# Hybrid decoder trunk on one core: the low part of one weight split per gate/up pair by an adding DMA

## The chip, the cores and the metric

The kernel runs on 1 core of one Trainium2 chip. The metric is device time of one execution in microseconds (us); the median of several runs is given. Engines are named as in the profile: PE (matmul) with PEld (its weight loads), DVE (vector), ACT (scalar), POOL (GpSimd), SP (which issues the DMAs of the kernel before).

## The reference

A two-layer decoder trunk in float32, run for a prompt of 512 tokens and for 8 samples of 8 tokens that share all weights, 576 token columns in all. Layer 0 mixes by causal pooling, layer 1 by a gated DeltaNet; each mixer is followed by a SwiGLU block:

```python
def swiglu(h, w_in, w_out):
    gu = h @ w_in
    return (jax.nn.silu(gu[..., :D_FF]) * gu[..., D_FF:]) @ w_out

for i in range(DEPTH):                      # DEPTH = 2, D_MODEL = 1024, D_FF = 2816
    h = rms_norm(x, norm_mix_pre[i])
    m = pool_mixer(...) if i % 2 == 0 else gdn_mixer(...)
    x = x + rms_norm(m, norm_mix_post[i])
    h = rms_norm(x, norm_ffn_pre[i])
    x = x + rms_norm(swiglu(h, ffn_w_in[i], ffn_w_out[i]), norm_ffn_post[i])
```

The outputs are the trunk's result for prompt and samples and the new states of both mixers.

## The kernel before

**Splits.** Every large matmul is done three times in a rounded 32-bit type (fp32r): a value x is held as a high part (x rounded to fp32r) and a low part (x less the high part), and the products high·high, high·low and low·high are summed. So each weight block is loaded (SP), copied to its high part (ACT) and subtracted to its low part (DVE or POOL, whichever the planner picks: `EITHER`). `split2` does it for two given tiles, `Weights.split` for tiles that it allocates.

**The gate/up pairs.** In each SwiGLU block, f runs over 22 blocks of 128 hidden columns. The first few (6 in layer 0, 5 in layer 1) are computed directly by `gate_up`; the other 33 (16 and 17) by the class `Strassen`, which takes the gate block and the up block of one f together, in seven products of half size. `Strassen.load` loads both 128x1024 weight blocks into tiles g (`graw`, two buffers) and u (`wraw`, three), forms sums of their halves, and splits three blocks of 128x1024 and one of 128x512: g itself to a (`wh`, `wl`), the half sum `s1raw` to s, then g after it was overwritten with two sums to b (tiles `dh` and `dl`, two buffers each), and u with its sum to c. `gated` runs the seven products in the order g1, g2, s2, s1, s3, s4, u2; s2 and s4 read b. Each product is 12 matmuls of 288 columns. In the profile the low part of b is the group `dl<-graw,dh`, the high part `dh<-graw`, and PE's use of them `ps_A<-ta,dl`, `ps_B<-hH,dh` and the like. Runs of pairs alternate with output projections: blocks of 6, 5, 4, 7 in layer 0 and 5, 5, 5, 7 in layer 1, where the first block is the direct one.

**The order of the work.** The program first records every operation in `Plan`. `Plan.cost` gives a planning price for each: how long it holds its engine, and when its result is there. `Plan.forward` then places the operations in time, engine by engine, by rank; where PE would be idle for long it inserts filling matmuls (`ps_w`). `Plan.refined` walks through the plan in windows of 60000 planned ns, in steps of 30000, and shifts ranks at random by the seeds that the constant `CHOSEN` lists for the window (`moved`); a string of `CHOSEN` is one such walk. The instructions are then emitted in the planned order. On the chip each engine runs its own instructions in that order and waits on semaphores, so the seeds fix the order on every engine, SP's DMA issues too. In the profile nearly all instructions have the one line that emits them; they are told apart by their tiles.

**Stretches** of the profiled execution, by the tiles in work: to about 100 us the pooling mixer, then layer 0's SwiGLU block with its pairs from 140 to 405, the DeltaNet layer from 440 to 1045, then the projection of its output and layer 1's direct blocks, its pairs from 1185 to 1455, and the end.

Of the kernel before, what the change touches and what calls it, by code (L numbers as in the profile page):

```python
# [20 lines left out]
P = 128  # L21
# [38 lines left out]
class Plan:  # L60
# [683 lines left out]
def hybrid_kernel(  # L744
# [147 lines left out]
    class Weights:  # L892
# [4 lines left out]
        def load(self, src, row, col, nk, n=P, eng=EITHER):  # L897
            raw = self.p.tile([P, 8, P], F32, name="wraw", tag="wraw", bufs=self.raw)[:, :nk, :n]
            SP.dma_start(raw, src[row:row + nk * P, col:col + n].rearrange("(k p) m -> p k m", p=P))
            return self.split(raw, eng)  # L900
# [1270 lines left out]
```

## Time and profile before

| what | value |
|---|---|
| median of 3 runs | 1513.48 us (1512.61 to 1514.94) |
| profiled execution, first to last instruction | 1513.1 us |
| granted clock of PE, mean | 0.997 |
| DMA share of the 16 engines, queue of SP | 45.1% |
| DMA packets of queue POOL | none |

The profiled execution's span lies 0.4 us below the median of the runs and inside their range. In the rows below, "busy" is the time in which an engine ran instructions (waiting and DMA issuing are not counted). A row of a group reads: line, engine, operation, tile written <- tiles read, shapes, count | busy us, mean ns of one | idle time of the engine just before, and what ended it. A row of the timeline reads: start us, us, engine, operation, tiles, and in brackets the idle time before it. Matmuls overlap, so a matmul's own duration is longer than the distance from one to the next.

### The profile page before, as it was taken

The numbers are of one execution on the slowest core, as the hardware profiler recorded it, in microseconds if no ns is written. First come the engines' busy times: TensorE is split into PE (matmuls) and PEld (weight loads), VectorE is DVE, ScalarE is ACT, GpSimd is POOL, SyncE is SP. The second block draws the span as 40 slices with busy tenths as digits, with TensorE's granted clock in tenths as the row PEclk, the third lists the DMA queues.
The fourth block names the chain that finished last, engine by engine and source line by source line (L and its number), as shares of the span: only waits on it lengthen the run. The fifth ranks groups of instructions, "written<-read, shape, count | busy, mean of one in ns | idle before, by whom it ended". The sixth has DMA issues, their size and how long they took to land.

```text
span 1513.1 us, 30285 instructions
## 1 busy us (share of the span) xinstructions
PE 1492.6 (99%) x11786; PEld 1446.6 (96%) x11786; DVE 1134.2 (75%) x2289; ACT 853.6 (56%) x1841; POOL 106.8 (7%) x240
## 2 busy tenths in 40 slices
PE   8999999999999999999999999999999999999998
PEld 7999999999999899899899899999999999999997
DVE  7993566668789697897899789557896485767856
ACT  7753443435555875774694784645565453533555
POOL 4100000000011010110121030000110000000000
PEclk9999999999999999999999999999999999999999
DMA  7564333233466443334443544657865332233264
GB/s 198 171 173 114 87 91 95 75 98 111 124 180 186 108 116 112 105 101 132 127 116 101 152 113 123 212 149 212 249 187 168 112 97 86 81 93 114 69 166 136
DMA packets 344934, 198.12 MB, mean 131 GB/s; under 512 B 13515, under 2 KB 337708, under 8 KB 344783
## 3 DMA queue, kind: packets, MB, share of 16 engines
q1 hardware_dynamic: 344791, 196.18, 45.1%
q8 instruction: 93, 1.52, 0.4%
q14 instruction: 50, 0.41, 0.1%
HBM read 165.86 MB, written 30.52 MB: 130 GB/s over the span
## 4 chain that ended last, share of the span: by engine, by line
PE 86%; DVE 6%; ACT 3%; DMA 3%; issue 1%; POOL 0%; SPq 0%; DVEq 0%; ACTq 0%; POOLq 0%
PE ps_A L462 27%; PE ps_B L462 26%; PE ps_m L462 19%; PE ps_s L462 5%; PE ps_k L462 5%; PE ps_x L462 2%; PE ps_e L462 1%; DVE wl L462 1%; DMA xt<-in_x_prompt_dram 1%; PE ps_n L462 1%; DVE y L462 1%; ACT wh L462 1%; DVE nacc L462 1%; PE ps_g L462 0%; ACT QD L462 0%
## 5 line engine op out<-in xcount | busy, mean ns | idle before, releaser
L462 DVE TENSOR_TENSOR wl<-wraw,wh 128x1024 fp32r<-128x1024 f32 (+4 forms) x238 | 266.2, 1123 | 76.4 <-ACT wh L462 47.3
L462 ACT ACTIVATE wh<-wraw 128x1024 fp32r<-128x1024 f32 (+4 forms) x239 | 232.4, 977 | 155.0 <-PE ps_B L462 65.3
L462 PE MATMUL ps_m<-hH,wh 128*128 128x320 f32 (+1 forms) x832 | 252.0, 315 | 0.7 <-ACT zz L462 0.4
L462 PE MATMUL ps_m<-hH,wl 128*128 128x320 f32 (+1 forms) x832 | 247.2, 309 | 0.0
L462 PE MATMUL ps_m<-hL,wh 128*128 128x320 f32 (+1 forms) x832 | 245.8, 306 | 0.1
L462 PEld LDWEIGHTS ps_m<-hH,wh 128*128 128x128 f32 x832 | 154.7, 189 | 4.1 <-ACT u L462 0.9
L462 PEld LDWEIGHTS ps_m<-hL,wh 128*128 128x128 f32 x832 | 155.3, 189 | 2.4 <-issue 0.8
L462 PEld LDWEIGHTS ps_m<-hH,wl 128*128 128x128 f32 x832 | 154.5, 189 | 2.7 <-issue 1.1
L462 PE MATMUL ps_B<-hL,wh 128*128 128x288 f32 (+2 forms) x444 | 129.1, 306 | 0.0
L462 PE MATMUL ps_B<-hH,wl 128*128 128x288 f32 (+2 forms) x444 | 128.4, 306 | 0.2
L462 PE MATMUL ps_B<-hH,wh 128*128 128x288 f32 (+2 forms) x444 | 128.4, 305 | 0.0
L462 PE MATMUL ps_A<-hH,wl 128*128 128x288 f32 (+2 forms) x432 | 117.9, 289 | 0.2
L462 PE MATMUL ps_A<-hH,wh 128*128 128x288 f32 (+2 forms) x432 | 117.4, 288 | 0.3 <-ACT nsq L462 0.3
L462 PE MATMUL ps_A<-hL,wh 128*128 128x288 f32 (+2 forms) x432 | 117.1, 288 | 0.0
L462 PE MATMUL ps_A<-aH,wl 128*128 128x288 f32 (+2 forms) x408 | 114.5, 297 | 0.0
L462 PE MATMUL ps_A<-aH,wh 128*128 128x288 f32 (+2 forms) x408 | 114.2, 298 | 0.0
L462 PE MATMUL ps_A<-aL,wh 128*128 128x288 f32 (+2 forms) x408 | 113.7, 296 | 0.0
L462 PE MATMUL ps_B<-aH,wl 128*128 128x288 f32 x296 | 83.3, 297 | 0.0
L462 PE MATMUL ps_B<-aH,wh 128*128 128x288 f32 x296 | 82.7, 295 | 0.3 <-ACT nsq L462 0.3
L462 PEld LDWEIGHTS ps_B<-hH,wl 128*128 128x128 f32 x444 | 81.8, 188 | 0.8 <-DVE wl L462 0.7
L462 PE MATMUL ps_B<-aL,wh 128*128 128x288 f32 x296 | 82.6, 294 | 0.0
L462 PEld LDWEIGHTS ps_B<-hL,wh 128*128 128x128 f32 x444 | 81.9, 188 | 0.1
(457 smaller groups left out, 3966.1 us busy)
## 6 DMA issues: line engine op xcount, KB each, us to landing
wraw<-in_ffn_w_in_dram SPq DMA_DIRECT2D x77, 512.0 KB
wraw<-in_gdn_w_in_dram SPq DMA_DIRECT2D x56, 512.0 KB
graw<-in_ffn_w_in_dram SPq DMA_DIRECT2D x33, 512.0 KB
wraw<-in_ffn_w_out_dram SPq DMA_DIRECT2D x32, 448.0 KB
wraw<-in_gdn_w_out_dram SPq DMA_DIRECT2D x24, 512.0 KB
wraw<-in_ffn_w_out_dram SPq DMA_DIRECT2D x32, 320.0 KB
St<-in_state_gdn_rec_dram SPq DMA_DIRECT2D x32, 256.0 KB
out_dram<-St SPq DMA_DIRECT2D x32, 256.0 KB
```

What stands on the lines that cost most here:

```text
L462: calls[e](*a, **k)
```

## The change

`split3` is new: ACT writes the negated high part (a copy with scale -1, rounded to fp32r) into the low tile, then the high part into the high tile, and POOL issues a DMA that reads the source and adds it onto the low tile. The subtraction on DVE is gone. `Strassen.load` uses `split3` in place of `split2` for b, the block in `dh` and `dl`. `Weights.load` and `Weights.split` take a new argument `adds` that nothing sets. `Plan.cost` gets a price for a DMA issued by POOL. `CHOSEN` is replaced: 6 strings with 4926 seeds in place of 4 strings with 2045.

```diff
     CHOSEN = (
-        "0: 30370 22361 86136 57126 4872 4820 4237 36728 5998 9791 48895 50747 41137; 1: 45223 42774 67949 96695 "
...
     )
...
         if method == "dma_start":
             m = n * list(out.ap)[0][1]
             flat = len(list(out.ap)) == 2
+            if eng == "POOL":
+                return 1000.0, 2500.0 + m * 4 / 240.0
...
-        def load(self, src, row, col, nk, n=P, eng=EITHER):
+        def load(self, src, row, col, nk, n=P, eng=EITHER, adds=False):
             raw = self.p.tile([P, 8, P], F32, name="wraw", tag="wraw", bufs=self.raw)[:, :nk, :n]
             SP.dma_start(raw, src[row:row + nk * P, col:col + n].rearrange("(k p) m -> p k m", p=P))
-            return self.split(raw, eng)
-
-        def split(self, raw, eng=EITHER):
+            return self.split(raw, eng, adds)
+
+        def split(self, raw, eng=EITHER, adds=False):
...
-            ACT.activation(h, raw, AF.Copy)
-            eng.tensor_tensor(l, raw, h.bitcast(F32), op=sub)
+            if adds:
+                split3(raw, h, l)
+            else:
+                ACT.activation(h, raw, AF.Copy)
+                eng.tensor_tensor(l, raw, h.bitcast(F32), op=sub)
             return h, l
...
+    def split3(src, hi, lo):
+
+        ACT.activation(lo, src, AF.Copy, scale=-1.0)
+        ACT.activation(hi, src, AF.Copy)
+        POOL.dma_start(lo, src, accum_op=add)
...
             b = tuple(ap_.tile([P, 8, P], F32R, name="d" + x, tag="d" + x, bufs=2) for x in "hl")
-            split2(g, *b)
+            split3(g, *b)
             c = w.split(u)
```

425 rows, old and new, of the table CHOSEN are left out of this document.

## The prediction

> **What bounds the kernel now.** I read the page's busy shares first, then busy time by stretch, then the chain, then single pairs of blocks in the timeline.
>
> ```profile
> span 1513.1 us, 30285 instructions
> PE 1492.6 (99%) x11786; PEld 1446.6 (96%) x11786; DVE 1134.2 (75%) x2289; ACT 853.6 (56%) x1841; POOL 106.8 (7%) x240
> ```
>
> TensorE is the bound; VectorE, which the change relieves, stands at 75%. Shares of a whole span hide stages, so here are stretches (window, its length, busy us and instructions of PE, PEld, DVE, ACT, POOL, granted clock, DMA share, GB/s):
>
> ```profile
> 0.00:100.00 100.00, 94.00 (x717) 89.45 (x718) 87.15 (x213) 71.69 (x158) 27.30 (x82) 1.00 0.67 185
> 140.00:405.00 265.00, 265.00 (x1997) 264.59 (x1996) 176.79 (x272) 116.28 (x179) 0.00 (x0) 1.00 0.31 90
> 440.00:1045.00 605.00, 598.11 (x5085) 560.71 (x5084) 492.97 (x1195) 400.38 (x1082) 64.67 (x142) 1.00 0.47 135
> 1045.00:1185.00 140.00, 139.79 (x1053) 138.48 (x1053) 106.45 (x195) 78.64 (x134) 11.47 (x12) 1.00 0.66 198
> 1185.00:1455.00 270.00, 270.00 (x2037) 269.75 (x2036) 187.14 (x289) 120.86 (x184) 0.00 (x0) 1.00 0.32 93
> 1455.00:1513.10 58.10, 50.73 (x380) 48.85 (x378) 34.47 (x58) 30.14 (x55) 0.00 (x0) 0.95 0.56 158
> ```
>
> The 33 gate/up pairs that the change touches lie in 140 to 405 and 1185 to 1455. PE is busy there for 265.00 of 265 and 270.00 of 270 us, 132.7 ns per matmul (265/1997); DVE is busy 67% and 69%, ACT 44% and 45%, POOL not at all. Where DVE is relieved, PE doesn't wait for it. PE's idle time is elsewhere: 6.0 us at the start, 6.9 us in the DeltaNet stretch (605 - 598.11), 7.4 us at the end, where the last transposes, norms and stores follow one another.
>
> ```profile
> 9.70 15.43 DMA xt<-in_x_prompt_dram
> 444.71 6.26 DMA wraw<-in_gdn_w_in_dram
> 1148.16 5.67 DMA wraw<-in_ffn_w_in_dram
> ...
> L458 PE MATMUL ps_w<-ones 128*128 128x128 f32 x86 | 13.9, 307 | 1.3 <-POOL ones L237 1.3
> ```
>
> The first three are pieces of the chain (start, us): a wait for the input at the start, and two waits for one 512 KB weight block. The last is a filling matmul, 86 of them, 13.9 us: PE time that is a wait too.
>
> **The change, part by part.** (Against 1513.1 us of span; the three runs have a median of 1513.48, so 0.4 us are added to the span.)
>
> ```profile
> L462 DVE TENSOR_TENSOR dl<-graw,dh 128x1024 fp32r<-128x1024 f32 x33 | 40.3, 1221 | 10.7 <-ACT dh L462 10.6
> L462 ACT ACTIVATE dh<-graw 128x1024 fp32r<-128x1024 f32 x33 | 34.8, 1054 | 31.1 <-DVE graw L462 29.1 <-PE ps_A L462 2.0
> q1 hardware_dynamic: 344791, 196.18, 45.1%
> ```
>
> 1. Removed: 33 subtractions of 1.221 us, 40.3 us of DVE. Worth 0: PE stands over them, idle 0.00 us in both stretches.
> 2. Added on ACT: 33 negated copies, the same copy as dh with a scale, so 33 x 1.054 = 34.8 us, 16 of them in the first stretch and 17 in the second: ACT rises from 116.3 to 133.2 of 265 and from 120.9 to 138.8 of 270. Cost 0, covered by ACT's idle half. They stand ahead of dh on ACT's queue, so dh is 1.05 us later, and the copies that free PSUM may queue behind them.
> 3. Added on POOL and the DMA engines: 33 adds of 512 KB. The DMA engines spent 45.1% of 1513.1 = 682 us on 196.18 MB, 3.48 us per MB, thus 1.8 us for 0.524 MB, 3.6 if the old value is read as well; 16 x 3.6 = 58 us lift the share in the first stretch from 0.31 to 0.53. PE loses 0.21 of 140 us where the share is 0.66, so this bandwidth costs 0.
> 4. How long one add takes isn't in the trace: no DMA is issued by POOL. From below it is bounded by what it replaces, 1.2 us. From above by the longest landing, 6.26 us, plus POOL's slowest small instruction beside a busy DVE:
>
> ```profile
> L462 POOL TENSOR_TENSOR sqs<-qks x10: 395/650/2034, 603.5 to 874.3; 128x128 f32<-128x128 f32 x10
> L462 POOL MEMSET Rs<- x4: 952/952/956, 589.5 to 950.4; 128x1024 f32 x4
> ```
>
> that is 6.26 + 2.03 = 8.3 us. I take 4.7 us, which is also the planner's price in the diff (2500 + 524288/240 ns): it lies above the bare 1.8 to 3.6 us and below the 5.67 us of a load in a stretch with twice the DMA traffic.
> With it dl comes 1.05 + 4.7 - 1.22 = 4.5 us later than now (1.0 at the low end, 8.1 at the high end). What waits for it:
>
> ```profile
> 282.40 1.22 DVE L462 TENSOR_TENSOR dl<-graw,dh 128x1024 fp32r<-128x1024 f32 x1
> 284.26 0.19 PEld L462 LDWEIGHTS ps_B<-ta,dl 128*128 128x128 f32 x1
> ...
> 361.42 1.06 ACT L462 ACTIVATE dh<-graw 128x1024 fp32r<-128x1024 f32 x1 [3.17 <-DVE graw L462]
> 362.63 1.22 DVE L462 TENSOR_TENSOR dl<-graw,dh 128x1024 fp32r<-128x1024 f32 x1
> 363.88 0.37 SPq L462 DMA_DIRECT2D graw<-in_ffn_w_in_dram  x1
> 363.91 0.19 PEld L462 LDWEIGHTS ps_A<-ta,dl 128*128 128x128 f32 x1
> 375.73 1.06 ACT L462 ACTIVATE wh<-graw 128x1024 fp32r<-128x1024 f32 x1 [0.26 <-PE ps_A L462]
> ...
> 1415.85 1.23 DVE L462 TENSOR_TENSOR dl<-graw,dh 128x1024 fp32r<-128x1024 f32 x1 [0.19 <-ACT dh L462]
> 1425.60 0.19 PEld L462 LDWEIGHTS ps_A<-hH,dl 128*128 128x128 f32 x1
> ```
>
> Three pairs: dl is done 0.64, 0.06 and 8.5 us before PE's first load of it. The order is just in time, so a late dl shows at once unless the new order starts it earlier. Room for that is there: d has two buffers, and between the last product that reads one pair's d (s4) and the first that reads the same buffer again (s2, two pairs on) stand ten products of 12 matmuls (u2, the seven of the pair between, g1, g2), 10 x 12 x 0.1327 = 15.9 us; copy, copy and add take 1.05 + 1.05 + 4.7 = 6.8. At 8.3 us it is 10.4, still inside. Cost 0 if the order uses it.
> 5. SP's queue: the next load into graw is issued when dl has read it (363.85, issue at 363.88); that release goes from DVE to the add's landing. The block loaded there is first read at 375.73, 11.9 us after the issue, and a landing takes up to 6.3 us, so 5.6 us are to spare against 4.5. Behind the waiting issue stand SP's other loads:
>
> ```profile
> SPq L462 <- DVE dl L462: 113.8, 18, 13.8
> ```
>
> SP waits for dl 18 times already, up to 13.8 us, with PE full. Cost 0, but this is the second thinnest cover. On POOL nothing queues behind the adds: it has no instruction in either stretch.
> 6. New seeds: the whole order is drawn again, everywhere. They can't win in the pair stretches. What an order can win is waits: 6.0 + 6.9 us idle and 13.9 us of filling, 26.8, less the 15.4 us of the input's wait: 11.4 us. They can lose as much as a bad order leaves, which the trace doesn't show. There are 4926 seeds for 2045, so I take a gain of a third, 3.8 us, between nothing and 11.4.
>
> Sum: 0 + 0 + 0 + 0 + 0 - 3.8: span 1509.3, time about 1509.5.
>
> **The rivals.**
> B: the adds are hidden and the order is worth nothing on the chip. For it: PE at 99%. Against: 11.4 us of waits are left. 1513.
> C: the adds land later than the order allows for, and PE stalls in the pair stretches. For it: two of the three leads above are under 0.7 us; the sqs row shows POOL work stretched five times (395 to 2034 ns). Against: the memset on POOL, which reads nothing, is even (952 to 956 ns). Six runs of pairs (blocks of 5, 4, 7 and 5, 5, 7) follow one another with projections between; once PE is late in a run, the rest of that run is no longer late. Between an overshoot of 0 and 8.3 - 4.7 = 3.6 us I take 1.8, less a lead of 0.4: 6 x 1.4 = 8 us, so 1513.5 + 8 = 1521 without a gain elsewhere, 1518 with it; I say 1519. It decides once the add overshoots by more than 3.8/6 + 0.4 = 1.0 us, at 5.7 us.
> The Trainium skill (SBUF — State Buffer, "SBUF: two separate sides") says that VectorE in a two-port mode locks GpSimd out of writing descriptors, with a DMA stretched from about 620 to 3100 ns; by that each add would be some 2.5 us late (an estimate from that page) and C would hold. The same section says that an instruction with two SBUF inputs locks out only GpSimd work that reads SBUF, by which C would fall away; the sqs and memset rows agree with the second half, and no run shows a descriptor being written.
> D: the order wins more than PE's idle time shows. The weight loader is idle for 605 - 560.71 = 44.3 us in the DeltaNet stretch, against 0.4 us in a pair stretch. A third of it, 14.8 us, gives 1499. Against: long passes of small matmuls leave the loader idle without a wait. The Trainium skill (Perfetto Trace Analysis, "Identifying the Most-Contended Engine") prefers the weight loads' busy share to the matmuls' as a measure of room; by it D's 44.3 us is the room, by the matmul row 6.9.
>
> **How the numbers follow.** My forecast (A) has 0.42, B 0.25, C 0.25, D 0.08. Three runs spread by 2.3 us, so 0.2% (3.0 us) is what can be told from no change: under 1510.5 is faster, over 1516.5 slower. Faster: 0.38 of A and D, 0.46. Same: the rest of A, most of B, a little of C, 0.28. Slower: most of C and the bad orders of B, 0.26. A's own range is 1505 to 1513; with B, most of C and the near half of D 1501 to 1521.
>
> **What would show it.** Right: PE busy for the full length of both pair stretches, DVE some 40 us lower, ACT 35 higher, 33 POOL issues of 512 KB, DMA share near 0.5 there; the gain, if any, in the start and the DeltaNet stretch. Step 4 is wrong if PE's loads of dl have idle time that ends with an add's landing, step 5 if graw's loads do, step 6 if the DeltaNet stretch is as long as before or longer. The prediction is wrong as a whole if an add takes more than 5.7 us from its issue, or if the new order is the worse one.

## The result, and the profile after

| kernel | median us (lowest to highest) | ratio to before, 95% interval |
|---|---|---|
| before | 1513.48 (1511.06 to 1515.01) | 1 |
| changed | 1519.16 (1516.6 to 1524.78, 6 runs) | 1.0043 [1.0027, 1.0059] |

The changed kernel is slower by 0.43%, some 6 us; the prediction had it 4 us faster. Its profiled execution is the shortest of the six (1516.6 us, span 1514.8). The five others have spans of 1516.0 to 1523.0 us, three of them with a mean granted clock of 0.995 or 0.996 against 0.998 (0.003 of 1520 us are 4.6 us).

From the page of the changed kernel: span, busy shares, DMA queues, and the new DMA (KB each, median us from issue to landing).

```profile
span 1514.8 us, 30474 instructions
...
PE 1486.2 (98%) x11784; PEld 1443.2 (95%) x11784; DVE 1103.5 (73%) x2247; ACT 885.7 (58%) x1874; POOL 139.5 (9%) x282
...
q1 hardware_dynamic: 344791, 196.18, 45.0%
q0 software_dynamic: 4752, 17.30, 6.0%
...
dl<-graw POOLq DMA_DIRECT2D x33, 512.0 KB, 5.5
```

The trade is made as described: DVE has 31 us less, ACT 32 us more, 33 adds move 17.30 MB. PE is busy 6.4 us less than before (1492.6), but idle 8.1 us more (28.6 for 20.5 of the span). The same stretches as before, by windows (the two pair stretches and the DeltaNet stretch between them):

```profile
140.00:405.00 265.00, 260.63 (x1961) 259.85 (x1960) 158.50 (x252) 128.53 (x191) 13.90 (x16) 1.00 0.47 120
440.00:1045.00 605.00, 598.24 (x5129) 563.10 (x5128) 498.45 (x1198) 406.39 (x1091) 68.80 (x153) 1.00 0.48 136
1185.00:1455.00 270.00, 268.63 (x2015) 267.23 (x2015) 166.05 (x266) 133.55 (x195) 14.56 (x17) 1.00 0.50 126
```

In the pair stretches PE was busy for 265.00 of 265 and 270.00 of 270 us; now 4.37 and 1.37 us are idle, 5.74 in all. The DeltaNet stretch holds 44 matmuls more in the same 605 us (5129 for 5085), about 5 us at 598/5129 us each, 1.7 of them the clock's (the execution of before has 3.4 us at half clock there): the new order does gain. What ended PE's waits, from the view of waits (total us, times, longest), and the low part's instructions from the view of that tile (ns least/median/longest):

```profile
PE ps_A L636 <- DMA dl<-graw: 2.7, 3, 2.0
PE ps_A L636 <- DVE y L636: 2.2, 1, 2.2
PE ps_B L636 <- DMA dl<-graw: 0.8, 3, 0.5
...
L636 POOL DMA_DIRECT2D dl<-graw x33: 850/859/1038, 152.6 to 1434.7; - x33
...
DMA to landing us min/median/max: 4.4/5.5/9.3
```

So 3.5 us of the 5.74 are waits for the low part, and one wait of 2.2 us (`y`, the sum of the output projections) is nearly all the rest; it is taken up below.

The add that the planner prices at 4.7 us lands after 4.4 at best, 5.5 in the median and 9.3 at worst. Ten of the 33 land 0.04 us before PE's first load of the low part: PE stands ready and starts on the landing. The longest one, in the chain of waits (start, us):

```profile
1411.62 0.96 ACT dl L636
1412.58 0.29 issue
1412.87 9.26 DMA dl<-graw
1422.12 0.04 issue
1422.17 0.93 PE ps_B L636 x5
```

Why this one takes 9.26 us and the one before it 4.39 is seen in the windows of just these two adds:

```profile
1407.79:1412.18 4.39, 4.39 (x36) 4.39 (x34) 4.25 (x9) 3.83 (x6) 0.86 (x1) 1.00 0.60 119
1412.87:1422.13 9.26, 9.14 (x69) 8.91 (x68) 5.49 (x10) 5.20 (x9) 0.86 (x1) 1.00 0.71 172
```

The last figure is GB/s: 4.39 us x 119 = 0.52 MB is the add and nothing else; 9.26 x 172 = 1.59 MB is the add and two weight blocks of 512 KB, which SP issued 0.56 us before it and 0.17 us after it. Whoever comes first is served first: in the first 4 us after the issue the loads (q1) moved 0.76 MB, the add (q0) a single packet.

```profile
q1 hardware_dynamic: 1497, 0.76, 68.6%
q0 software_dynamic: 1, 0.00, 0.5%
```

The add's first packet moves 3.84 us after its issue, alone after 1.43. Over all 33, the 14 adds with no byte of SP's queue beside them have a median of 4.43 us (4.38 to 5.68), the 13 with more than 500 KB beside them 6.93 (5.51 to 9.26). The four of the 14 that take 5.0 to 5.7 us each have a packet of the instruction queues (q8, q14; 8 or 16 KB) beside them, and so have two that take 4.5 and 4.6; the other eight take 4.38 to 4.44.

It goes the other way too. The wait of 2.2 us for `y` ends a chain that begins with a weight block (start, us):

```profile
321.19 6.35 DMA wraw<-in_ffn_w_in_dram
...
328.97 0.82 DVE y L636 x2
```

SP issued this load 0.98 us after an add (320.21), and in the first 3.6 us only the add's packets moved. VectorE waits for the block, `y` stands behind it in VectorE's order, and PE waits for `y`. In other runs of this same order, below, the same load lands after 4.68 us (adds in halves), 4.10 (half of the work by the add), 4.16 (no accumulation) and 3.73 (no adds), and PE waits for `y` 0.5 us in the first of them and not above 0.3 in the others.

### The profile page after: what moved, and what is told of

The parts are those of the page before. It is cut to its first block, busy times and chain, and to the rows that moved or that the text cites. A ratio compares the mean times of both kernels' runs of the same rounds, so it can differ in the third digit from the quotient of the medians.

```text
span 1514.8 us, 30474 instructions
## 1 busy us (share of the span) xinstructions
PE 1486.2 (98%) x11784; PEld 1443.2 (95%) x11784; DVE 1103.5 (73%) x2247; ACT 885.7 (58%) x1874; POOL 139.5 (9%) x282
## 3 DMA queue, kind: packets, MB, share of 16 engines
q0 software_dynamic: 4752, 17.30, 6.0%
## 4 chain that ended last, share of the span: by engine, by line
PE 81%; DVE 6%; DMA 5%; issue 5%; ACT 3%; POOL 0%; DVEq 0%; SPq 0%; ACTq 0%; POOLq 0%
PE ps_A L636 24%; PE ps_B L636 23%; PE ps_m L636 19%; PE ps_s L636 5%; PE ps_k L636 5%; DMA dl<-graw 3%; PE ps_x L636 2%; DVE wl L636 1%; PE ps_e L636 1%; PE ps_n L636 1%; ACT wh L636 1%; DMA wraw<-in_ffn_w_in_dram 1%; DMA graw<-in_ffn_w_in_dram 1%; DVE y L636 1%; DVE vt L636 0%
## 5 line engine op out<-in xcount | busy, mean ns | idle before, releaser
L636 PE MATMUL ps_m<-hH,wl 128*128 128x320 f32 (+1 forms) x832 | 242.5, 307 | 0.0
L636 PE MATMUL ps_B<-aL,wh 128*128 128x288 f32 x296 | 85.8, 295 | 0.0
L636 PEld LDWEIGHTS ps_B<-hH,wh 128*128 128x128 f32 x444 | 82.1, 188 | 0.5 <-ACT wh L636 0.5
```

The lines of the kernel that those rows point to most:

```text
L636: calls[e](*a, **k)
```

## The experiments

The leading theory: the order of the changed kernel is good, and its loss is the adds that land after the time the order allows, together with the load that an add holds up. Rivals: the order itself is worse; the software queue costs something by being used; POOL's issue is stretched by a busy VectorE.

**The order without the adds.** The order of the changed kernel; VectorE subtracts as before, at the planned end of the high copy, and ScalarE writes no negated copy.

```diff
-        ACT.activation(lo, src, AF.Copy, scale=-1.0)
         ACT.activation(hi, src, AF.Copy)
-        POOL.dma_start(lo, src, accum_op=add)
+        nc.vector.tensor_tensor(lo, src, hi.bitcast(F32), op=sub)   # put into the finished order
```

> The changed kernel's order on every engine, but the low part of b comes from DVE again: the negated copy is left out and a subtraction stands in DVE's order where the high part is planned to be done. Late adds: in the changed kernel PE stood idle 4.4 us in the first pair stretch and 1.4 us in the second, in a profiled execution (1516.6) that was the fastest of six; with the subtraction both stretches are full and the time is 1516.6 - 5.8 - some 1.4 outside the span = 1509 to 1511, with a spread like that of the kernel before (4 us, not 8). Bad order: the new order is the loss by itself, 1516 or more. Fixed cost of the software queue alone: 1517.5.

Measured: 1511.76 us, ratio 0.9995 [0.9986, 1.0003]. Its pair stretches:

```profile
140.00:405.00 265.00, 264.06 (x1985) 262.71 (x1985) 178.29 (x272) 116.95 (x178) 0.00 (x0) 1.00 0.32 93
1185.00:1455.00 270.00, 267.90 (x2011) 266.88 (x2010) 184.00 (x284) 118.61 (x176) 0.00 (x0) 1.00 0.33 95
```

No low part comes within 2 us of PE's read. The order isn't the worse one; this rival is out. But the stretches are not full, as the expectation had them: 0.94 and 2.10 us are idle, and 3.4 us of PE's waits end with ScalarE's `nh` (a copy that frees a PSUM bank), against 0.5 in the changed kernel. Nor is the 3.8 us gain there while VectorE still has its 33 subtractions; that this order had no place for them is likely, not shown.

**The adds without the order.** The order of before; ScalarE's negated copy goes in ahead of the high copy, the add takes the subtraction's place.

```diff
-            split2(g, *b)
+            split3(g, *b)      # emitted at split2's places in the order of before
```

> The kernel before with its own order, and only the adding DMA put in: the negated copy right ahead of the high part on ACT, the DMA on POOL where DVE subtracted. Late adds: an add lands 5.5 us after its issue, so dl is some 4.5 us later than DVE had it; a run of pairs pays that less its smallest lead, leads of 1.8, 0.6, 0.1, 1.4, 1.5 and 2.2 us in the six runs: 19.7 us in all, 1533 us, idle time of PE in the pair stretches that ends with an add's landing. Bad order: this order is the good one, so 1513 to 1515.

Measured: 1597.76 us, ratio 1.0562 [1.0546, 1.0578], 65 us above what was expected. Windows and waits:

```profile
140.00:405.00 265.00, 238.78 (x1697) 234.28 (x1696) 136.80 (x218) 108.50 (x163) 11.32 (x13) 0.96 0.40 102
1185.00:1455.00 270.00, 252.51 (x1819) 249.11 (x1818) 144.57 (x224) 115.76 (x172) 9.44 (x11) 0.97 0.43 115
```
```profile
PE ps_B L468 <- DMA dl<-graw: 22.1, 13, 3.4
PE ps_A L468 <- DMA dl<-graw: 20.1, 10, 3.6
```

PE waits for 23 of the 33 adds, 42.2 us; so a late pair does not shelter the next. The clock falls too: its mean is 0.984, so (0.998 - 0.984) x 1593.6 = 22 us more are lost at reduced speed. With ScalarE's copies (11.5 us by a run below) that makes 76 of the 84 us, if the three simply add up; the other 8 are not traced. These adds land sooner than the changed kernel's (median 4.4 against 5.5): 18 of them have no byte of a load beside them, where the changed kernel has 14.

**One late add, one early add.** The order of before, a single add, the rest as before: in the 31st pair, then in the first.

```diff
+        if plan.pairs not in (30,):     # the second kernel: (0,)
+            split2(src, hi, lo)
+            return
```

> The kernel before with one add alone, in the 31st pair, where dl was ready 8.5 us before its first use; the other 32 low parts stay on DVE. Late adds: nothing waits, 1513.5. Fixed cost of using the software queue (the changed kernel's time stands 1.8 us above its span): about 1515.

The 31st pair had been chosen for the 8.5 us of room that the prediction read there; it has 0.28 (step 4 below). Measured: 1516.57 us, ratio 1.0021 [1.0012, 1.003], 3.4 us. Two 10 us windows around it, the wait, and two shorter windows:

```profile
1410.00:1420.00 10.00, 7.18 (x45) 6.71 (x44) 4.04 (x7) 4.24 (x6) 1.03 (x1) 0.86 0.43 98
1420.00:1430.00 10.00, 10.00 (x74) 10.00 (x74) 4.80 (x8) 3.45 (x6) 0.00 (x0) 0.97 0.26 77
```
```profile
PE ps_B L468 <- DMA dl<-graw: 2.1, 1, 2.1
```
```profile
1413.86:1417.27 3.41, 1.03 (x6) 0.56 (x5) 1.59 (x2) 1.14 (x2) 0.30 (x1) 1.00 0.77 154
1417.27:1420.68 3.41, 2.97 (x12) 2.97 (x13) 0.00 (x0) 0.17 (x1) 0.00 (x0) 0.50 0.44 116
```

PE waits 2.1 us, and then the granted clock is 0.86 and 0.97 in the two longer windows: (0.14 + 0.03) x 10 = 1.7 us are lost, by a stretch of 3.4 us at half speed. It is the last window shown, and it begins 0.4 us before the wait ends, so 0.2 us would be counted twice: 2.1 + 1.5 = 3.6 us for one late add of 4.5 us. The Trainium skill (TensorE: Matmul & The Clock Gate, "Part 1: The HAM clock gate (the "warmup" mystery)") has the half-rate state follow an idle window of about 3.4 us; the length of the slow stretch agrees, while here a wait of 2.1 us was enough.

Not every such wait is followed by a slow stretch: in the changed kernel's profiled execution the waits of 2.0 and 2.2 us were not. In these traces the slow stretches begin at whole multiples of 3.413 us after the first clock record: here (1417.27 - 4.15) / 3.413 = 414.0, in the run with all adds (195.82 - 4.67) / 3.413 = 56.0. Cut by this grid as in the two shorter windows (in the first PE is idle for 3.41 - 1.03 = 2.38 us), each of the 14 full-speed windows in the pair stretches in which PE is idle for 1.835 us or more (eleven in the run with all adds, one in each of three others) is followed by a slow stretch, and none with 1.828 us or less; the changed kernel's two waits leave 1.78 and 1.83 us in their windows. So the same wait can cost its own length or some 1.5 us more, by its place on the grid. That three of the changed kernel's other executions have a lower mean clock fits this, but their profiles are not on record.

> The kernel before with one adding DMA, in the first gate/up pair instead of the 31st: there the subtraction is done 8.4 us before the tensor engine first loads the low part. If a late landing and the clock after it are all that an add costs, this one costs nothing: 1513.1, ratio 0.999 to 1.001, while the one in the 31st pair (0.3 us of room) cost 3.4. If using the software queue at all costs something once in a run (its first use, its descriptors), this one costs as much as that one did: 1516.5, ratio 1.002.

Measured: 1513.4 us, ratio 1.0007 [0.9998, 1.0017]. An add with 8.4 us of room costs nothing that can be told from zero, and a first use of the software queue neither. The room decides.

**Each add as two of 256 KB**, the half that PE reads first (s2) in front; the order of the changed kernel.

```diff
-        POOL.dma_start(lo, src, accum_op=add)
+        for q in (slice(0, KQ), slice(KQ, NC)):
+            nc.gpsimd.dma_start(lo[:, q], src[:, q], accum_op=add)
```

> The changed kernel with each add issued as two of 256 KB, the half that s2 reads first. Late adds: the first half lands earlier (about 4 us instead of 5.5), s4 reads the second three products later, so PE's idle time in the pair stretches falls by half and the time to 1515 to 1517. If it is POOL's issuing or a fixed part that makes an add long, the halves take as long as the whole and the time stays at 1519 or rises to 1522.

Measured: 1509.39 us, ratio 0.9973 [0.9964, 0.9982]: faster than before, 9.8 us faster than the changed kernel.

```profile
140.00:405.00 265.00, 264.01 (x1990) 263.45 (x1990) 162.44 (x259) 131.49 (x195) 28.12 (x32) 1.00 0.50 126
1185.00:1455.00 270.00, 269.28 (x2023) 268.68 (x2022) 168.17 (x269) 134.17 (x196) 27.95 (x32) 1.00 0.52 129
```
```profile
PE ps_A L640 <- DMA dl<-graw: 0.5, 1, 0.5
PE ps_B L640 <- DMA dl<-graw: 0.4, 1, 0.4
```

This is better than expected. The bytes are the same, POOL's issues are doubled, and PE's waits for the low part fall from 3.5 to 0.9 us: the half that is read first lands earlier. The wait for `y` falls from 2.2 to 0.5 us, as the weight block behind the add lands after 4.68 us instead of 6.35. These two waits are 4.3 of the 8.2 us between the two profiled spans (1514.8 and 1506.6); where the rest goes is not traced.

**The same transfer without accumulation.** This leaves the low part unsubtracted.

```diff
-        POOL.dma_start(lo, src, accum_op=add)
+        POOL.dma_start(lo, src)
```

> The changed kernel with a plain copy in the adding DMA's place: the same 512 KB, source, destination and queue, without the accumulation, so the low part is left unsubtracted. If the accumulation itself is what makes the landing long (the destination is read before it is written), the copy lands in clearly less than the add's 4.4 / 5.5 / 9.3 us (least, median, longest), about 3.5 in the median, the tensor engine's waits for it fall from 3.5 us to under 1 and the time to about 1510. If the landing is set by the other traffic and by the queue, the copy lands as the add does, 5.2 to 5.5 us in the median with about 9 at the longest, and the time is that of the changed kernel, 1515 to 1519.

Measured, one execution: 1509.45 us. DMA queue, issue and landing, windows:

```profile
q0 software_dynamic: 4752, 17.30, 3.4%
```
```profile
L636 POOL DMA_DIRECT2D dl<-graw x33: 530/530/734, 153.4 to 1427.5; - x33
...
DMA to landing us min/median/max: 2.8/3.7/5.7
```
```profile
140.00:405.00 265.00, 264.94 (x1999) 264.54 (x1998) 161.80 (x259) 131.04 (x195) 8.69 (x16) 1.00 0.42 127
1185.00:1455.00 270.00, 269.96 (x2029) 269.55 (x2028) 168.33 (x269) 133.94 (x196) 8.48 (x16) 1.00 0.44 130
```

The accumulation costs 1.6 us of the least landing (4.4 to 2.8) and 1.8 of the median; the engines' time per transfer is 3.4% x 1507.7 / 33 = 1.55 us against 6.0% x 1514.8 / 33 = 2.75. A transfer that lands within the planner's 4.7 us most times (24 of 33) lets PE run both stretches all but full. The Trainium skill (DMA: Bandwidth & Descriptors, "Anatomy of one DMA — SWDGE (gpsimd) path") fits 2.0 us + bytes/436e3 to a DMA from GpSimd, by estimate 3.2 us here: near the copy's 2.8, too low for the add's 4.4, since the fit has no term for accumulating.

**More traffic beside the add.** A 512 KB copy of graw to a scratch buffer on ScalarE's queue, ahead of the negated copy, then behind it.

```diff
+        nc.scalar.dma_start(to, src)    # second kernel: after the next line
         ACT.activation(lo, src, AF.Copy, scale=-1.0)
```

> The changed kernel with a second transfer beside every add: ScalarE's queue sends the same 512 KB graw tile to a scratch buffer in device memory, issued just ahead of the negated copy, about 1 us before the add. If other transfers that move at the same time are what makes an add land late, its landing rises to 6.5 to 8 us in the median (from 5.5), and the least, 4.4, rises too; more of the 33 adds end the tensor engine's wait, and the time goes above 1522. If each queue has its own share and the long landings come from something else (the issue, the place in the run), the landing stays at 5.3 to 5.8 and the time at 1515 to 1519.

Measured, one execution: 1525.85 us; landing 4.4 / 5.6 / 9.0, PE's waits for the low part 11.0 us.

> The changed kernel with a second 512 KB transfer beside every add, as in the earlier run with the scratch buffer, but issued from ScalarE's queue just behind the negated copy instead of ahead of it, so that it moves while the add does. If transfers that run at the same time are what lengthens an add, the adds that have no weight load beside them, 4.4 us in all runs so far, land at 5.5 to 6.5 us here, the median goes from 5.5 to above 6.2, and the time above 1522. If an add's landing depends only on the weight loads of SyncE's queue, these adds stay at 4.4 to 4.6 us and the time at 1515 to 1519.

Measured, one execution: 1524.64 us; landing 4.4 / 5.8 / 10.3, waits 11.9 us.

```profile
PE ps_A L639 <- DMA dl<-graw: 6.4, 4, 3.0
PE ps_B L639 <- DMA dl<-graw: 5.5, 6, 1.8
```

The times went as contention has them, the landings only in part: the 14 adds with no weight load beside them stay at 4.4 us in the median. For twelve of them the extra copy was over within 1.5 us of the add's issue, when the add's first packet is about to move (1.43 us where nothing is ahead); it was too early to collide. For the two where it moved until 1.9 and 2.5 us, the add landed later: the 28th 5.12 to 5.52, the 18th 5.68 to 6.33. Of the 13 that had more than 500 KB of loads beside them, eleven landed 0.3 to 2.2 us later (the 12th 7.27 to 8.80, the 24th 6.93 to 9.17), the first stayed, and the 19th landed 1.1 us earlier, with 0.22 MB of loads beside it where it had 0.71. So it's the queueing behind loads that lengthens an add, and one more transfer mostly lengthens it further; a transfer that doesn't overlap does next to nothing. The load that holds up `y` takes 6.38 us in the second of these runs, and PE waits 2.3 us. The Trainium skill (DMA: Bandwidth & Descriptors, "SWDGE vs HWDGE vs iDMA") says that each DMA engine takes turns between its queues; the two rows of q1 and q0 above do not show it (0.76 MB of loads against one packet of the add in 4 us), so here the measurement decides.

**The trade of engines alone.** The order of before, the 33 subtractions left out, ScalarE's negated copies put in, no DMA.

```diff
-        EITHER.tensor_tensor(lo, src, hi.bitcast(F32), op=sub)
+        nc.scalar.activation(lo, src, AF.Copy, scale=-1.0)    # ahead of the high copy
```

> The kernel before, its order kept, with the 33 subtractions left out and ScalarE writing the negated copy ahead of the high one in every pair; nothing is added onto it, so the low part of these splits is not computed. This is the trade of engines alone, 40.3 us off VectorE and 34.8 us onto ScalarE, without a new order and without a DMA. The prediction gave both a worth of 0 in the order of before: 1512 to 1514, ratio 0.999 to 1.001. If VectorE's subtractions end waits of the tensor engine in the old order (three leads of them are under 0.3 us), it is faster, 1509 to 1511. If ScalarE's copies come in the way, it is slower, 1515 and more.

Measured: 1525.53 us, ratio 1.008 [1.0066, 1.0094]. Windows, and what PE now waits for:

```profile
140.00:405.00 265.00, 260.18 (x1941) 257.32 (x1941) 156.91 (x251) 127.83 (x191) 0.00 (x0) 1.00 0.30 86
1185.00:1455.00 270.00, 267.34 (x2005) 265.58 (x2004) 164.63 (x263) 133.21 (x197) 0.00 (x0) 1.00 0.30 88
```
```profile
PE ps_A L468 <- ACT nh L468: 3.1, 5, 1.1
PE ps_B L468 <- ACT nh L468: 1.8, 4, 1.0
```

ScalarE is half idle and the trade still costs 11.5 us. `nh` stands behind the new copy on ScalarE's queue, and the matmul that needs the bank waits up to 1.1 us: 4.9 us in all, where it was 0.4 before. Both stretches together have 7.5 us of idle time; the rest of the 11.5 is not traced to a wait. In the changed kernel the wait for `nh` is 0.5 us in all. In the old order, then, the trade costs 11.5 us that a new order has to win back before it gains anything.

**Half of it by the add.** The order of the changed kernel; VectorE subtracts the half that is read first, GpSimd adds the other.

```diff
+        nc.scalar.activation(lo[:, q], src[:, q], AF.Copy, scale=-1.0)        # q: second half
         ACT.activation(hi, src, AF.Copy)
+        nc.vector.tensor_tensor(lo[:, p], src[:, p], hi[:, p].bitcast(F32), op=sub)
+        nc.gpsimd.dma_start(lo[:, q], src[:, q], accum_op=add)
```

> The changed kernel's order, with the work on the low part divided: VectorE subtracts the half that the tensor engine reads first (128x512, into s2), and only the other half (256 KB, read two products later) is negated by ScalarE and added from GpSimd. If late landings are the whole of the changed kernel's loss, no product waits for a DMA any more, the matmuls of both pair stretches run as in the run with two halves or better, and the time is 1508 to 1510, ratio 0.996 to 0.998. If the subtractions that come back to VectorE cost what they cost in the run with all 33 of them in this order (1511.8, some 2.3 us above the run with two halves), half of it comes back: 1510.5, ratio 0.998. 1513 or more would mean that something other than the landings holds the order up.

Measured: 1508.28 us, ratio 0.9974 [0.9962, 0.9986], level with the two halves and better than both kernels.

```profile
140.00:405.00 265.00, 264.75 (x1998) 264.42 (x1997) 172.48 (x275) 125.51 (x195) 13.91 (x16) 1.00 0.42 111
1185.00:1455.00 270.00, 269.44 (x2022) 268.58 (x2021) 177.89 (x286) 129.34 (x198) 13.73 (x16) 1.00 0.44 113
```

No product waits for the low part, the load that held up `y` lands after 4.1 us, the whole loss is gone, and the 22 us of VectorE that come back (33 x 0.684) cost nothing that shows. With the run of two halves it settles where the loss comes from: whole adds of 512 KB that collide with weight loads, which makes the add late for its product and the load late for its own. The two runs relieve both at once, so what each is worth is known only from the waits of the profiled execution, 3.5 and 2.2 us. Not tried: a new search of the order with the add priced as it lands.

## Why the prediction was wrong, point by point

1. *Subtractions removed, worth 0.* Not resolved by itself; in the new order all 33 cost about 2.4 us (1511.8 without adds against 1509.4 with adds in halves), 33 halves nothing that shows.
2. *ScalarE's copies, cost 0.* Right for the changed kernel only because its order was drawn again. In the old order they cost 11.5 us net of the subtractions, in part by the path that the step names (copies that free PSUM queue behind them) and then doesn't price. A half-idle engine was taken as cover; its queue order is not.
3. *Bandwidth, cost 0.* The shares came as estimated (0.47 and 0.50 for 0.53). But the sentence asked only how long PE idles in a stretch whose DMA is busy, and this zero is wrong too. The add loses by the loads: 4.4 us alone, 6.9 in the median beside more than 500 KB of them. And a load loses by an add: 6.35 us for a block that takes 3.7 to 4.7 in other runs of the order, for which PE waited 2.2 us in the end.
4. *An add of 4.7 us, hidden.* **The step that failed.** The bounds, 1.2 and 8.3, were nearly right (4.4 to 9.3 measured), but the value taken was the price that the order itself was made with, and the order leaves little room above that price: twelve of the 14 adds with no weight load beside them land only 0.5 to 2.1 us ahead of PE's read, and ten of the 33 land when PE is already there. Those ten are what the runs showed in place of "hidden": 3.5 us of waits in the profiled execution. The order doesn't keep the room of ten products. One of the three quoted leads was misread: for the pair of 1415.85 I gave 8.5 us, to a product of the other bank. Products of neighbouring blocks interleave, and the first read stands here, in the timeline of before:

```profile
1417.35 0.19 PEld L462 LDWEIGHTS ps_B<-ta,dl 128*128 128x128 f32 x1
```

0.28 us after the subtraction (1415.85 + 1.23 = 1417.08). So all three quoted leads were short, and the room that I saw in one of them is not there.
5. *SP's queue, cost 0.* Held, as far as it goes: the late release of `graw` delays nothing that PE reads (the delayed load of step 3 is another tile's, late in landing and not in issue: it leaves 0.98 us behind the add here and in the run of halves). SP now waits 205.4 us for the low part's tile where it was 113.8, and no wait of PE ends with `graw`.
6. *New order, -3.8 us.* About right in size, when the adds are in time: -3.7 (1509.4) and -4.6 (1508.3) against the runs of before taken with them. Part of that is luck: it was to come from PE's waits, but PE's idle time in the DeltaNet stretch is 6.9 us before and 6.8 now, and the filling matmuls are 86 and 84. What fell there, besides the 1.7 us of slow clock, is the idle time of the weight loader, 44.3 to 41.9 us, which is rival D's measure, though far from D's 14.8. In the changed kernel the gain is covered by the loss of steps 3 and 4, some 10 us.

The small term "0.4 us around the span" was wrong too: span and time of the profiled executions differ by 1.8 us each time (1516.6 and 1514.8; 1508.1 and 1506.3). The profiled execution of before thus took 1514.9 us, 1.4 above the median.

Rival C (1519) is what happened, by its mechanism and near its time, at a chance of 0.25. Its threshold, a landing of 5.7 us, lies between the median of 5.5 and the mean of 5.75. Its arithmetic does not hold, so the nearness of its time is luck: it let each run of pairs pay once, but the run with the adds in the old order shows 23 of 33 pairs paying, and it had no term for the load that an add delays, nor for the clock, which can add 1.5 us to a wait of 2. The lock between VectorE and GpSimd (the Trainium skill, SBUF — State Buffer, "SBUF: two separate sides") is not the reason: VectorE is busy 60% of these stretches and POOL's 33 issues take 850 to 1038 ns, with no stretched one among them, as the second half of that rule has it.

## What to carry to other kernels

When work moves to a DMA, ask for the spread of its landing beside the transfers that will really be there, and compare it with the lead in the order as planned; here a schedule that was optimised with one price had little margin above it. Ask too which loads are issued just behind it. Where the consumer reads the result in parts, send the part that is read first by itself, or leave that part where it was. And take "half idle" as cover for an in-order engine only after naming what stands behind the new instruction on its queue.

## What the runs showed of the hardware

- A 512 KB accumulating DMA within the on-chip memory, issued by GpSimd: 4.4 us alone (eight adds, 4.38 to 4.44), 5.5 in the median of the changed kernel and up to 9.3 beside loads; without accumulation 2.8, 3.7 and 5.7; as 256 KB 3.2 at the least. The issue takes GpSimd 0.86 us with and 0.53 us without accumulation.
- Of two transfers on different queues the one that was there first went first: beside two weight blocks an add moved one packet in 4 us while they moved 0.76 MB, and a 512 KB load issued 0.98 us behind an add moved nothing for 3.6 us and landed after 6.35.
- In the pair stretches TensorE's granted clock went to half for 3.41 us or twice that, always at a multiple of 3.413 us from the first clock record: after each full-speed window of that grid with 1.835 us or more of idle time (14 windows, four runs), after none with 1.828 or less. By this count a wait of 2.1 us cost 3.6 us in one run, and two waits of 2.0 and 2.2 us cost only themselves in another. The limit does not hold for other stretches: in the DeltaNet stretch of the kernel before, a window with 0.75 us of idle time was followed by half speed, and at the end of the program one with 0.83.
